# Six of eight row tiles of an output projection as block products of seven multiplications

## The chip, the cores and the metric

The kernel runs on one core of a Trainium2 chip. The metric is device time in microseconds of one execution, the median of several runs. Engines are named as the profile names them: TensorE (PE, with its weight loads PEld), VectorE (DVE), ScalarE (ACT), GpSimd (POOL) and SyncE (SP), which here only issues loads.

## The reference

A two-layer encoder works on 512 positions of 1024 channels, in float32. Each layer has an FFN, a token mixer and a second FFN, and the part that changes is the mixer's last matrix product:

```python
h = rmsnorm(x, g_mix[l])
p = h @ w_in[l]
gates = jax.nn.sigmoid(p[..., OFF_G:].astype(jnp.float32)).astype(x.dtype)
gates = gates.reshape(b, s, N_BRANCHES, d)
y_f = fourier_mix(p[..., OFF_F:OFF_B], w_fourier[l])
y_c = short_conv(p[..., OFF_B:OFF_C], p[..., OFF_C:OFF_V], p[..., OFF_V:OFF_P], w_conv[l], w_conv_out[l])
y_p = pool_mix(p[..., OFF_P:OFF_G], w_pool[l], pool_scale[l])
merged = gates[:, :, 0] * y_f + gates[:, :, 1] * y_c + gates[:, :, 2] * y_p
x = x + merged @ w_o[l]
...
h = rmsnorm(x, g_ffn2[l])
x = x + 0.5 * swiglu(h, w1_b[l], w3_b[l], w2_b[l])
```

## The kernel before

Activations lie transposed: channels on the 128 partitions, positions along the row. x is eight tiles of 128 x 512, merged likewise, and each is called a row tile. Every float32 operand is split into a high and a low part (parth and partl for weights; mergedh, unit, n and so on for activations), and a product is three matmuls: high by high, high by low, low by high (lines 362 to 364, function mm).

Most products are not made tile by tile. A job takes two output columns of the weight and pairs of row tiles, and computes the resulting 2 x 2 blocks (two row tiles by two halves of 256 positions) with seven products of blocks, M1 to M7, where a plain product needs eight. Sums of blocks replace the eighth. On the weights' side those sums are formed by VectorE in Weights.step ("sums", "rest"); on the activations' side by operands (for a normed x, tiles n) or transform (for other tiles, tiles unit). The results of the products are added by VectorE, either into temporary tiles (take) or directly to x (added). Jobs of the FFN's down projection (w2) are of the latter kind: downwards(job) says so. They use three pairs of row tiles.

run goes through the jobs. Each job issues M1 and M5, then the previous job's M4, M6, the previous job's M3, M2, M7. After the last job run issues the pieces of `after`, between them the last M4 and M3. Small pieces of VectorE and ScalarE work wait in the list `later`, of which each product issues one; a product that needs operands not yet made issues from the list until they are. A framework then orders the instructions of each engine by its own estimate and gives buffers out: 50 units of 128 x 528 in the pool act for all activations' parts.

In the mixer, jobs compute the input projection. The kinds are f, c and p for the three gates of two row tiles each, "cv" and "b" for the convolution's inputs, and "pool". Behind a gate job follow the matmuls of its branch (fourier, convolved, pooling). The function gated multiplies by the gate and adds; after gate c, rows 2i and 2i+1 of merged are complete and split_later makes their parts. The projection w_o then runs tile by tile in columns: 64 pieces (eight output columns by eight row tiles), each of three matmuls of 512 positions. The last two row tiles are held back in the first four columns. When a column is complete, finish adds it to x (line 1096), and next_norm makes the normed operand hh and hl (lines 379, 380) and the square b (line 388). POOL adds squares of columns 1 to 6 into a running sum (line 390); the buffer b has two copies.

The next FFN begins with lead: wide matmuls with hh and hl. After four row tiles of its first column it calls mean_squares (matmuls of line 404 on the summed squares, then VectorE and POOL make the norm's factor), later spread (line 430 on ScalarE) and operands (lines 476 to 494), whose tiles n the first jobs of the FFN need.

Weights come by DMA on SP's queue. A Layout fixes from an estimated time line when each is loaded and split. Kinds "raw" and "last" of a job, and chunks marked added, get their low part by a second, accumulating DMA on POOL's queue (line 207); plain chunks get it by VectorE (line 194). The projection's weights were plain chunks.

Of the kernel before, what the change touches and what calls it, by code (L numbers as in the profile page):

```python
# [13 lines left out]
ALU = mybir.AluOpType  # L14

P = 128
# [6 lines left out]
KD = D // P  # L23
# [8 lines left out]
MAXW = 1024  # L32
AW = 528
UNITS = 50
LEAD, PHASE, PLAIN = 3, 6, 18
WARM = 10


# [268 lines left out]
def encoder(ctx: ExitStack, tc: tile.TileContext, layout, x_in, w_in, consts_in, gain_in, out):  # L307
# [25 lines left out]
    def col(name, l, k):  # L333
        o = COLS[name] + l * (CW[name]) + k
        return cst[:, o : o + 1]

    def psum():
        return psp.tile([P, S], F32, tag="ps", name="ps")
# [21 lines left out]
    def mm(ps, a, b, start, stop, more=False):  # L360
        (ah, al), (bh, bl) = a, b
        nc.tensor.matmul(ps, ah, bh, start=start, stop=False, skip_group_check=more)  # L362
        nc.tensor.matmul(ps, ah, bl, start=False, stop=False, skip_group_check=more)  # L363
        nc.tensor.matmul(ps, al, bh, start=False, stop=stop, skip_group_check=more)  # L364
# [4 lines left out]
    state, later = {}, []  # L369

    ps = psum()
# [64 lines left out]
    def tt(out, a, b, op=ALU.mult):  # L436
        nc.vector.tensor_tensor(out=out, in0=a, in1=b, op=op)  # L437
# [91 lines left out]
        ))  # L529

    def downwards(job):
        return job[0][0][:2] == "w2"

    def added(job, which, ps):

# [343 lines left out]
    def mix(l, after):  # L879
# [85 lines left out]
        def gate(kind, i, rest):  # L965
            o = OFF_G + {"f": 0, "c": 1, "p": 2}[kind] * D + 2 * i * P
            job(kind, i, o, o + P, rest)

        branch = {}

        def pooling(m):
            while m // 2 not in pooled:
                one()
            branch[m] = psum()
            mm(branch[m], weights.tile(("w_pool", l, 0, m * P, P)), pooled[m // 2], True, True)

        def convolved(m, k):
            while k not in conv:
                one()
            if k == 0:  # L980
                branch[m] = psum()
            mm(branch[m], weights.tile(("w_conv_out", l, k * P, m * P, P)), conv[k], k == 0, k == 3)

        for i in range(4):
            gate("f", i, [lambda m=m: fourier(m) for m in (2 * i, 2 * i + 1)])
# [10 lines left out]
        def pool_gate(i):  # L996
            gate("p", i, [lambda m=m: pooling(m) for m in (2 * i, 2 * i + 1)])

        for do, i in (
            (pool_in, 0), (conv_in, 0), (pool_in, 2), (pool_gate, 0), (conv_in, 1), (conv_gate, 0), (pool_gate, 1),  # L1000
            (conv_in, 2), (pool_gate, 2), (conv_in, 3), (conv_gate, 2), (pool_gate, 3),
        ):
            do(i)
        for i in range(4):
            ms = (2 * i, 2 * i + 1)
            gate("c", i, [lambda m=m, k=k: convolved(m, k) for ks in ((0, 1, 2), (3,)) for m in ms for k in ks])

        def shifted(i, z):
# [13 lines left out]
        def gated(kind, m, s):  # L1022

            if kind == "f":
                tt(yf[m], yf[m], s)
            elif kind == "p":
                nc.vector.scalar_tensor_tensor(
                    out=s, in0=branch.pop(m), scalar=col("pool_scale", l, m), in1=s,
                    op0=ALU.mult, op1=ALU.mult,
                )  # L1030
                tt(yf[m], yf[m], s, ALU.add)
            else:
                tt(s, branch.pop(m), s)
                tt(s, yf.pop(m), s, ALU.add)
                split_later("merged", s, merged, m)

        def take(job, which, ps, addend, late):
            kind, i = kinds[job]
            first, c = which[0] == "1", slice(0, Q) if which[1] == "1" else slice(Q, S)
            if which == "11":  # L1040
# [54 lines left out]
        def finish(m, ps):  # L1095
            tt(x[m], ps, x[m], ALU.add)
            after(m)

        run(jobs, take, (), columns("w_o", l, merged, range(KD), finish, 4, 2), between)
        state.pop("n")  # L1100

    def next_norm(gain, l):
# [105 lines left out]
```

## Time and profile before

| what | value |
|---|---|
| runs | 2036.67, 2030.64, 2034.03 us; median 2034.03 |
| profiled execution | 2033.19 us |
| its span, first to last instruction | 2031.4 us |
| mean granted TensorE clock | 0.990 |
| projection w_o, layer 0 | 635.7 to 682.7 us of the span |
| mean matmuls behind it (line 404) | from 688.5 us |

The sums of the prediction stand against the profiled execution and are then carried over to the median of the runs. In the rows of groups, the figures after the bar are busy time and mean length of one, then the idle time before and what ended it. In rows of the timeline, the first two numbers are start and length in microseconds. A row of waits has the total, the count and the longest.

### The profile page before, as it was taken

How to read it: one execution, taken by the hardware profiler on the slowest of the kernel's cores; microseconds unless marked ns; L12 is line 12 of the kernel's file. 1: busy time of each engine (PE TensorE's matmuls, PEld its weight loads, DVE VectorE, ACT ScalarE, POOL GpSimd, SP SyncE). 2: the span in 40 equal slices, each digit the busy share in tenths (PEclk: the TensorE clock that was granted, in tenths of full speed). 3: DMA queues.
4: the chain of work that ended last, by engine and by line, in shares of the span. 5: the costliest groups of instructions: out<-in, count | busy, mean ns of one | idle time of the engine just before them, and what ended most of it. 6: DMA issues, size and time to landing. Idle time of an engine off the chain costs nothing.

```text
span 2031.4 us, 38426 instructions
## 1 busy us (share of the span) xinstructions
PE 1989.9 (98%) x14886; PEld 1898.5 (93%) x14886; DVE 1547.5 (76%) x2595; ACT 1364.6 (67%) x2250; POOL 455.5 (22%) x532
## 2 busy tenths in 40 slices
PE   8999999899999999999999999998999999999998
PEld 6899999799998899999979999988999988999997
DVE  5888887788875588888768888868897656788884
ACT  6767667776665676766667667677766556766764
POOL 3321212311110422122241212232111123121120
PEclk8999999999999999999999999999999999999999
DMA  9787878767875778787977978887787667687872
GB/s 252 155 195 172 208 165 226 160 140 168 190 174 160 155 148 195 172 207 165 228 153 152 210 166 201 183 202 154 164 182 185 164 168 141 148 209 175 194 173 89
DMA packets 145623, 358.00 MB, mean 176 GB/s; under 512 B 16160, under 2 KB 36000, under 8 KB 145440
## 3 DMA queue, kind: packets, MB, share of 16 engines
q0 software_dynamic: 59184, 149.99, 44.9%
q1 hardware_dynamic: 86112, 205.31, 31.1%
q8 instruction: 116, 1.90, 0.4%
q14 instruction: 67, 0.55, 0.1%
q10 hardware_dynamic: 144, 0.24, 0.0%
HBM read 340.80 MB, written 2.10 MB: 169 GB/s over the span
## 4 chain that ended last, share of the span: by engine, by line
PE 87%; DMA 3%; ACT 3%; issue 2%; DVE 2%; POOL 2%; POOLq 0%; SPq 0%; ACTq 0%; DVEq 0%
PE ps L363 29%; PE ps L362 29%; PE ps L364 29%; DMA n<-t 1%; DMA z<-weights 1%; DMA raw<-weights 1%; ACT parth L208 1%; ACT b L388 1%; POOL b L390 1%; DVE t L476 1%; ACT hh L379 1%; DMA w<-weights 1%; DVE t L437 0%; POOL n L489 0%; ACT partl L206 0%
## 5 line engine op out<-in xcount | busy, mean ns | idle before, releaser
L363 PE MATMUL ps<-n,parth 128*128 128x256 f32 x2760 | 779.1, 282 | 13.4 <-DMA n<-t 9.0
L362 PE MATMUL ps<-n,parth 128*128 128x256 f32 x2760 | 777.8, 282 | 5.7 <-ACT half L935 5.7
L364 PE MATMUL ps<-n,partl 128*128 128x256 f32 x2760 | 776.2, 281 | 0.0
L363 PEld LDWEIGHTS ps<-n,parth 128*128 128x128 f32 x2760 | 523.2, 190 | 16.3 <-DMA n<-t 10.3
L362 PEld LDWEIGHTS ps<-n,parth 128*128 128x128 f32 x2760 | 522.9, 189 | 7.5 <-ACT half L935 6.1
L364 PEld LDWEIGHTS ps<-n,partl 128*128 128x128 f32 x2760 | 523.0, 190 | 0.0
L207 POOL DMA_DIRECT2D part22l<-weights x163 | 143.2, 878 | 1038.5 <-ACT part22l L206 459.6
L208 ACT CAST part22h<-w 128x512 fp32r<-128x512 f32 (+1 forms) x163 | 96.1, 589 | 294.9 <-PE ps L363 198.7
L194 DVE TENSOR_TENSOR partl<-raw,parth 128x1024 fp32r<-128x1024 f32 (+3 forms) x217 | 242.8, 1121 | 40.0 <-ACT parth L193 39.7
L207 POOL DMA_DIRECT2D partl<-weights x200 | 175.9, 880 | 345.8 <-ACT partl L206 196.1
L363 PE MATMUL ps<-unit,parth 128*128 128x256 f32 x864 | 242.6, 281 | 0.0
L362 PE MATMUL ps<-unit,parth 128*128 128x256 f32 x864 | 242.6, 281 | 0.0
L364 PE MATMUL ps<-unit,partl 128*128 128x256 f32 x864 | 242.1, 280 | 0.0
L208 ACT CAST parth<-raw 128x1024 fp32r<-128x1024 f32 (+2 forms) x200 | 197.7, 988 | 50.2 <-PE ps L363 38.5
L193 ACT CAST parth<-raw 128x1024 fp32r<-128x1024 f32 (+3 forms) x217 | 207.9, 960 | 30.9 <-PE ps L363 29.4
L437 DVE TENSOR_TENSOR x<-ps,x 128x256 f32<-128x256 f32 (+1 forms) x376 | 164.0, 448 | 76.4 <-PE ps L364 76.3
L206 ACT ACTIVATE partl<-raw 128x1024 fp32r<-128x1024 f32 (+2 forms) x200 | 200.1, 1001 | 15.2 <-DMA raw<-weights 7.3
L239 DVE TENSOR_TENSOR raw<-raw,z 128x1024 f32<-128x1024 f32 (+1 forms) x163 | 186.2, 1143 | 23.0 <-ACT partl L206 16.3
L194 DVE TENSOR_TENSOR partl<-z,parth 128x1024 fp32r<-128x1024 f32 (+1 forms) x163 | 185.7, 1139 | 1.4 <-ACT parth L193 1.4
L437 DVE TENSOR_TENSOR b<-ps,sM 128x256 f32<-128x256 f32 x222 | 93.1, 420 | 117.2 <-PE ps L364 117.1
L584 ACT COPY sM<-ps 128x256 f32<-128x256 f32 x345 | 126.9, 368 | 77.0 <-PE ps L364 75.1
L193 ACT CAST parth<-z 128x1024 fp32r<-128x1024 f32 (+1 forms) x163 | 160.7, 986 | 15.1 <-PE ps L363 9.8
(188 smaller groups left out, 4052.3 us busy)
## 6 DMA issues: line engine op xcount, KB each, us to landing
raw<-weights SPq DMA_DIRECT2D x187, 512.0 KB, 4.6
partl<-weights POOLq DMA_DIRECT2D x146, 512.0 KB, 6.5
z<-weights SPq DMA_DIRECT2D x115, 256.0 KB, 3.9
w<-weights SPq DMA_DIRECT2D x115, 256.0 KB, 3.5
part22l<-weights POOLq DMA_DIRECT2D x115, 256.0 KB, 4.5
raw<-weights SPq DMA_DIRECT2D x50, 384.0 KB, 4.0
partl<-weights POOLq DMA_DIRECT2D x50, 384.0 KB, 5.7
n<-t POOLq DMA_DIRECT2D x48, 256.0 KB, 4.9
```

The lines of the kernel that those rows point to most:

```text
L193: self.nc.scalar.copy(hi[:, :w], src)
L194: self.tail.append((self.t, self.made, lambda: self.nc.vector.tensor_tensor(out=lo[:, :w], in0=src, in1=hi[:, :w].bitcast(F32), op=ALU.sub ...
L206: self.nc.scalar.activation(lo[:, :w], src, AF.Copy, scale=-1.0)
L207: self.nc.gpsimd.dma_start(lo[:, :w], self.source(key), accum_op=ALU.add)
L208: self.nc.scalar.copy(hi[:, :w], src)
L239: v.tensor_tensor(out=raw, in0=raw, in1=raws.pop(("third", key))[:, : 2 * w], op=ALU.subtract)
L362: nc.tensor.matmul(ps, ah, bh, start=start, stop=False, skip_group_check=more)
L363: nc.tensor.matmul(ps, ah, bl, start=False, stop=False, skip_group_check=more)
L364: nc.tensor.matmul(ps, al, bh, start=False, stop=stop, skip_group_check=more)
L379: nc.scalar.activation(pair[0], x[k], AF.Copy, scale=g)
L437: nc.vector.tensor_tensor(out=out, in0=a, in1=b, op=op)
L584: nc.scalar.copy(b["s" + q], ps)
```

## The change

The row tiles 0 to 5 of merged are now paired. When both tiles of a pair are complete, transform makes their seven operands, and four jobs of three pairs each (two output columns per job) are put behind the mixer's last gate job; their products are added to x by VectorE. Tiles 6 and 7 stay with columns, of which the last is held back. The gate job p 3, with its pooling, moves from before gate c 0 to before gate c 3, so the pooling and convolution results get keys of their own.

```diff
-LEAD, PHASE, PLAIN = 3, 6, 18
+LEAD, PHASE, PLAIN, MIXED = 3, 6, 18, 6
...
     def downwards(job):
-        return job[0][0][:2] == "w2"
+        return job[0][0] in ("w2_a", "w2_b", "w_o")
...
-        branch = {}
+        branch, done = {}, set()
+        state["g"] = {}
...
-            (conv_in, 2), (pool_gate, 2), (conv_in, 3), (conv_gate, 2), (pool_gate, 3),
+            (conv_in, 2), (pool_gate, 2), (conv_in, 3), (conv_gate, 2),
         ):
             do(i)
         for i in range(4):
             ms = (2 * i, 2 * i + 1)
+            if i == 3:
+                pool_gate(i)
             gate("c", i, [lambda m=m, k=k: convolved(m, k) for ks in ((0, 1, 2), (3,)) for m in ms for k in ks])
...
             else:
-                tt(s, branch.pop(m), s)
-                tt(s, yf.pop(m), s, ALU.add)
-                split_later("merged", s, merged, m)
+                tt(s, branch.pop((kind, m)), s)
+                tt(yf[m], yf[m], s, ALU.add)
+                if m >= MIXED:
+                    split_later("merged", yf.pop(m), merged, m)
+                elif m ^ 1 in done:
+                    transform(yf.pop(m & ~1), yf.pop(m | 1), state["g"], m // 2)
+                done.add(m)
 
         def take(job, which, ps, addend, late):
+            if downwards(job):
+                return added(job, which, ps)
...
-        run(jobs, take, (), columns("w_o", l, merged, range(KD), finish, 4, 2), between)
+        jobs += [(("w_o", l, m * P), ("w_o", l, (m + 1) * P), (0, MIXED // 2)) for m in range(0, KD, 2)]
+        run(jobs, take, (), columns("w_o", l, merged, range(MIXED, KD), finish, 4, 1), between)
```

On ScalarE, where the columns of layer 0's projection are finished, this is the order before. x_86 to x_93 are the row tiles 0 to 7 of x; hh is the normed operand and b the square; parth and partl are parts of weights.

```order
L379 ACTIVATE hh<-x_90,cst 128x512
L388 ACTIVATE b<-x_90 128x512
L208 CAST parth<-raw 128x1024
L206 ACTIVATE partl<-raw 128x1024
L379 ACTIVATE hh<-x_91,cst 128x512
L388 ACTIVATE b<-x_91 128x512
L193 CAST parth<-z 128x1024
L379 ACTIVATE hh<-x_92,cst 128x512
L388 ACTIVATE b<-x_92 128x512
```

And this is the same place in the changed kernel.

```order
L379 ACTIVATE hh<-x_90,cst 128x512
L193 CAST parth<-z 128x1024
L388 ACTIVATE b<-x_90 128x512
L379 ACTIVATE hh<-x_91,cst 128x512
L206 ACTIVATE partl<-raw 128x1024
L388 ACTIVATE b<-x_91 128x512
L379 ACTIVATE hh<-x_92,cst 128x512
L208 CAST parth<-raw 128x1024
L379 ACTIVATE hh<-x_93,cst 128x512
L388 ACTIVATE b<-x_92 128x512
L206 ACTIVATE partl<-raw 128x1024
L388 ACTIVATE b<-x_93 128x512
```

The squares b, which follow their operand hh directly before, now stand one to three instructions behind it, with conversions of weights between.

On VectorE, around the last gate job of layer 0, the order before is as follows: a and b are the two tiles of a gate, sM a kept product, yf the sum of the branches.

```order
L437 TENSOR_TENSOR a<-ps,sM_7929 128x256
L437 TENSOR_TENSOR b<-yf,b 128x512
L194 TENSOR_TENSOR partl<-raw,parth 128x1024
L437 TENSOR_TENSOR mergedl<-b,mergedh 128x512
L194 TENSOR_TENSOR partl<-raw,parth 128x1024
L437 TENSOR_TENSOR a<-ps,a 128x512
L437 TENSOR_TENSOR a<-yf,a 128x512
L437 TENSOR_TENSOR b<-ps,sM_7874 128x256
L437 TENSOR_TENSOR mergedl<-a,mergedh 128x512
```

In the changed kernel VectorE has this there; unit are the transform's tiles.

```order
L437 TENSOR_TENSOR a<-ps,sM_7982 128x256
L437 TENSOR_TENSOR unit<-yf,unit 128x256
L437 TENSOR_TENSOR unit<-yf,unit 128x512
L194 TENSOR_TENSOR partl<-raw,parth 128x768
L437 TENSOR_TENSOR unit<-unit 128x512
L232 TENSOR_TENSOR z<-z,w_7963 128x384
L437 TENSOR_TENSOR unit<-unit 128x512
L437 TENSOR_TENSOR unit<-yf,unit 128x256
L233 TENSOR_TENSOR z<-z,raw 128x384
L1030 SCALAR_TENSOR_TENSOR b<-ps,cst,b 128x512
```

The splits of merged (mergedl) have given way to the transforms of earlier pairs and to the sums of the new jobs' weights.

More of the change, by code (lines that the diff above doesn't have):

```diff
@@ L973, in pooling @@
                 one()
-            branch[m] = psum()
-            mm(branch[m], weights.tile(("w_pool", l, 0, m * P, P)), pooled[m // 2], True, True)
+            branch["p", m] = psum()
+            mm(branch["p", m], weights.tile(("w_pool", l, 0, m * P, P)), pooled[m // 2], True, True)
         def convolved(m, k):
@@ L980, in convolved @@
             if k == 0:
-                branch[m] = psum()
-            mm(branch[m], weights.tile(("w_conv_out", l, k * P, m * P, P)), conv[k], k == 0, k == 3)
+                branch["c", m] = psum()
+            mm(branch["c", m], weights.tile(("w_conv_out", l, k * P, m * P, P)), conv[k], k == 0, k == 3)
         for i in range(4):
@@ L1027, in gated @@
                 nc.vector.scalar_tensor_tensor(
-                    out=s, in0=branch.pop(m), scalar=col("pool_scale", l, m), in1=s,
+                    out=s, in0=branch.pop((kind, m)), scalar=col("pool_scale", l, m), in1=s,
                     op0=ALU.mult, op1=ALU.mult,
```

## The prediction

> **What bounds the kernel now.** I read the page first (busy time, chain), then TensorE's timeline for the pace of its instructions, the view of the merged tiles, a table of windows, and what TensorE waits for.
>
> ```profile
> span 2031.4 us, 38426 instructions
> PE 1989.9 (98%) x14886; PEld 1898.5 (93%) x14886; DVE 1547.5 (76%) x2595; ACT 1364.6 (67%) x2250; POOL 455.5 (22%) x532
> PE 87%; DMA 3%; ACT 3%; issue 2%; DVE 2%; POOL 2%; POOLq 0%; SPq 0%; ACTq 0%; DVEq 0%
> ```
>
> TensorE is busy for 98% of the span and holds 87% of the chain, so TensorE time saved in a stage without gaps comes off the end, as long as nothing else becomes late. Busy time is no price for a matmul, since matmuls overlap. The timeline gives the distance between starts:
>
> ```profile
> 589.76 0.28 PE L363 MATMUL ps<-n,parth 128*128 128x256 f32 x1
> ...
> 599.20 0.39 PE L362 MATMUL ps<-convh,parth 128*128 128x512 f32 x1
> ...
> 604.75 0.28 PE L362 MATMUL ps<-n,parth 128*128 128x256 f32 x1
> ```
>
> Between the first two rows stand 80 starts of 256 columns: 9.44 / 80 = 0.118 us each. Between the second and third stand 24 of 512 columns: 5.55 / 24 = 0.2315 us. The output projection runs at that pace in layer 0:
>
> ```profile
> L362 PE MATMUL ps<-mergedh,parth x64: 388/394/402, 635.7 to 682.3; 128*128 128x512 f32 x64
> L364 PE MATMUL ps<-mergedh,partl x64: 388/393/399, 636.2 to 682.7; 128*128 128x512 f32 x64
> ```
>
> 192 wide matmuls, with 24 narrow ones of the last gate job among them, start within 47.0 us: (47.0 - 24 x 0.118) / 191 = 0.231. No gap there. Next, windows: an FFN stage whose w2 products the new code copies, the stretch of the gate jobs, the projection.
>
> ```profile
> 110.00:147.00 37.00, 37.00 (x316) 37.00 (x315) 31.36 (x59) 23.36 (x35) 8.83 (x10) 1.00 0.89 210
> 573.70:635.50 61.80, 61.80 (x434) 57.59 (x433) 44.18 (x62) 37.27 (x61) 6.16 (x7) 1.00 0.67 175
> 635.50:683.00 47.50, 47.50 (x219) 39.07 (x218) 21.68 (x27) 24.63 (x34) 13.70 (x11) 1.00 0.60 150
> ```
>
> The columns are length, PE, PEld, DVE, ACT, POOL, granted clock, DMA share, GB/s. The clock is full. VectorE has 26 us to spare in the projection and 18 in the gate stretch. From 560 to 730 us TensorE waits only behind the next FFN's lead:
>
> ```profile
> PE ps L363 <- DMA n<-t: 1.7, 1, 1.7
> PE ps L363 <- DVE n L437: 1.3, 1, 1.3
> ```
>
> **The change, part by part.**
>
> TensorE. Each layer loses 48 pieces of 3 wide matmuls (six row tiles, eight columns): 144 x 0.2315 = 33.3 us. It gains 4 jobs x 7 products x 3 pairs x 3 matmuls = 252 narrow ones: 252 x 0.118 = 29.7 us. That is 3.6 us per layer and 7.2 in all. (One eighth would be 4.2; 0.6 is lost because two narrow ones take 0.236.) A rule speaks against this exchange: the Trainium skill (TensorE: Matmul & The Clock Gate, "Back-to-back issue gap") states some 131 ns for a 512-column matmul in a sustained stream. With it the removed work would be only 144 x 0.131 = 18.9 us, and the change would lose 10.8 us per layer, ending near 2055.7. The rows above measure 231 ns in this very stage, so I give that case no chance.
>
> VectorE. These rows price it (mean ns of one after the comma):
>
> ```profile
> L194 DVE TENSOR_TENSOR partl<-raw,parth 128x1024 fp32r<-128x1024 f32 x156 | 190.8, 1223 | 39.4 <-ACT parth L193 39.1
> L437 DVE TENSOR_TENSOR x<-ps,x 128x256 f32<-128x256 f32 x336 | 136.5, 419 | 43.4 <-PE ps L364 43.4
> L437 DVE TENSOR_TENSOR unit<-unit 128x512 fp32r<-128x512 f32 x108 | 74.0, 685 | 2.2 <-ACT unit L517 2.0
> L437 DVE TENSOR_TENSOR unit<-unit 128x256 f32<-128x256 f32 x144 | 57.4, 418 | 0.0
> L239 DVE TENSOR_TENSOR raw<-raw,z 128x768 f32<-128x768 f32 x48 | 45.9, 956 | 2.3 <-ACT parth L208 0.9
> L232 DVE TENSOR_TENSOR z<-z,w 128x384 f32<-128x384 f32 x48 | 26.4, 551 | 0.0
> ```
>
> Per layer: 28 additions to x at 0.42 (+11.7); weights of four jobs, each three passes of 768 columns at 0.95 and two of 384 at 0.55 (+15.8); six chunks of 1024 saved at 1.22 (-7.3); three pair transforms, each five passes of 256 and three of 512, against two passes of 512 before (+8.3). Sum +28.5 us per layer, against 44 spare (26 + 18), which hide it where they lie at the right place; were VectorE fully loaded, all 28.5 would show.
>
> The tight place lies before the first product. The unit buffers run out (28 operand tiles n stay until the last gate job), so the transforms bunch up in that job. There VectorE has 35 instructions between the "12" sum of gate c 2 and the last operand that product M1 needs. Instructions that wait for nothing overlap a little, as these three starts show (0.33 us apart, each 0.42 long):
>
> ```profile
> 698.62 0.42 DVE L437 TENSOR_TENSOR t<-t 128x256 f32<-128x256 f32 x1
> 698.95 0.42 DVE L437 TENSOR_TENSOR n<-t,n 128x256 fp32r<-128x256 f32 x1
> 699.29 1.22 DVE L239 TENSOR_TENSOR raw<-raw,z 128x1024 f32<-128x1024 f32 x1
> ```
>
> So the 35 take 18.3 us back to back (each some 0.085 less than its mean), 21.3 by the means. TensorE meanwhile has 114 narrow and 30 wide matmuls: 13.5 + 6.9 = 20.4 us. The ends are therefore 0 and 0.9 us late per layer; I take 0, because the w2 window shows VectorE 85% busy (31.36 of 37.00) with no wait on TensorE, and 18.3 / 0.85 = 21.5 would be 1.1 late at worst. In the four jobs VectorE has 28.6 us of work in TensorE's 36.0, 79%: 0. The moved gate job p 3 is the filler that makes this room; it issues the same instructions, and its loads on SP and accumulations on POOL move behind those of c 0 to c 2, as TensorE's need does. The conv products that it used to precede now follow their inputs directly, with 5.1 us of TensorE work (12 narrow of M2, 12 of M7, ten wide) against 4.2 of VectorE (two of 1024, two of 512, two of 256): 0, with a margin of only 0.9.
>
> ScalarE's rows:
>
> ```profile
> L193 ACT CAST parth<-raw 128x1024 fp32r<-128x1024 f32 x156 | 162.9, 1045 | 30.9 <-PE ps L363 29.4 <-DMA raw<-weights 0.7 <-PE ps L364 0.3
> L517 ACT CAST unit<-unit 128x512 fp32r<-128x512 f32 x108 | 65.7, 619 | 2.2 <-DVE unit L437 2.2
> L193 ACT CAST parth<-z 128x768 fp32r<-128x768 f32 x48 | 40.1, 836 | 2.1 <-PE ps L363 0.3
> ```
>
> It gains 12 casts (nine at 0.62, three at 0.42) and loses six at 0.62; each job has four weight passes of 768 at 0.84 and two of 384 (half of that, an estimate) against six of 1024 at 1.05 per layer: 3.1 + 16.8 - 6.3 = +13.6 us, into stretches where it is busy 37.27 of 61.80 and 24.63 of 47.50: 0. Neither this nor the next item removes a wait, so nothing can be gained. SP gets 6 more loads per layer. POOL gets 8 more accumulating DMAs per layer, 0.88 us of issue each:
>
> ```profile
> L207 POOL DMA_DIRECT2D partl<-weights x200 | 175.9, 880 | 345.8 <-ACT partl L206 196.1
> ```
>
> Behind them wait only later accumulations. That is 7 us on a queue busy 13.70 of 47.50, and at most the DMA share of 0.89 of the w2 window, where TensorE never waited: 0.
>
> The tail is where I see a cost. Before, each of the columns 4 to 7 took 24 wide matmuls, 5.6 us, so the squares were added at leisure. Now eight columns finish in 8.7 us (three wide, nine narrow, six wide, four times six wide after x0: 33 x 0.2315 + 1.06). POOL's six adds follow a loop: two buffers b, so the next square waits for the last add. The end of an FFN shows that loop when it is pressed, in DVE, POOL, ACT and PE rows:
>
> ```profile
> 1009.23 2.08 DVE L437 TENSOR_TENSOR x<-ps,x 128x512 f32<-128x512 f32 x3 [1.71 <-PE ps L364]
> 1016.64 1.30 POOL L390 TENSOR_TENSOR b<-b 128x512 f32<-128x512 f32 x1 [0.74 <-ACT b L388]
> 1020.82 0.63 ACT L388 ACTIVATE b<-x 128x512 f32<-128x512 f32 x1 [1.55 <-POOL b L390]
> 1027.85 1.84 PE L404 MATMUL ps<-mean,b 128*128 128x1 f32 x16
> L390 POOL TENSOR_TENSOR b<-b x6: 1298/1312/2057, 1011.8 to 1023.6; 128x512 f32<-128x512 f32 x6
> L390 POOL TENSOR_TENSOR b<-b x6: 1337/1524/1842, 660.2 to 679.7; 128x512 f32<-128x512 f32 x6
> L404 PE MATMUL ps<-mean,b x16: 166/250/250, 688.5 to 690.1; 128*128 128x1 f32 x16
> ```
>
> From the first column's addition (1009.2) to the end of the sixth add (1023.6 + 1.3) the FFN needs 15.7 us, and its mean matmuls come 3 us later. In layer 0's projection the adds ended at 681.5, 7 us ahead of 688.5. In the changed order the mean matmuls stand 28 wide matmuls behind the lead's start, so 8.7 + 6.5 - 0.2 = 15.0 us after x0. The chain needs 15.7, plus about 1.0 for one more weight conversion on ScalarE and one more DMA issue on POOL in it, which partly overlap: 16.7. TensorE runs in order, so the lead's matmuls and all that use them stand behind this wait: 1.7 us per layer, 3.4 in all. Ends: the bare loop, 2.6 + 5 x (0.74 + 1.30) + 1.3 = 14.1, gives 0; every add as long as the longest gives 1.7 + 5 x 0.75 = 5.4. What follows (spread, operands, the 3.0 us of waits behind the lead) keeps its order and its distance from the mean matmuls: 0.
>
> Sum: -7.2 + 3.4 = -3.8 us. Against the profiled execution (2033.19, span 2031.4) that is 2029.4; the median shown is 0.84 higher, so 2030.2.
>
> **The rivals.**
>
> Tail hidden. If the squares keep up, the full 7.2 us stay: 2026.8. For it speaks the FFN's 3 us of slack; against it, that columns here finish in half of an FFN's 2.8 us (twelve wide matmuls).
>
> VectorE late before the first product, which ends slower. At the tight place VectorE and ScalarE pass tiles back and forth in order. The gate jobs show such stops:
>
> ```profile
> 606.76 1.23 DVE L239 TENSOR_TENSOR raw<-raw,z 128x1024 f32<-128x1024 f32 x1 [3.10 <-ACT partl L206]
> 610.02 0.69 DVE L437 TENSOR_TENSOR a<-ps,a 128x512 f32<-128x512 f32 x1 [2.03 <-ACT a L1058]
> ```
>
> If both return there, 18.3 + 3.1 + 2.0 = 23.4 against 20.4: 3.0 us late per layer, 2036.2. It decides from 1.9 us per layer. Against it: VectorE had nothing else to do at these stops.
>
> POOL's adds lengthened by VectorE: all six at 2.06 cost 5.4 us per layer, so 2034.0 - 7.2 + 10.8 = 2037.6. One of six was that long in the FFN tail, and VectorE is denser now. The Trainium skill (SBUF — State Buffer, "Who interferes with whom") states the mechanism: a VectorE instruction with two SBUF inputs shuts out a GpSimd instruction that reads SBUF for its whole length; 2057 against 1298 ns agrees, but the other rows show that it rarely meets.
>
> The saving swallowed: if the operands behind the lead come no earlier in time, its 3.0 us of waits grow and 2034 stays. Against it: that chain starts at the mean matmuls.
>
> **How the numbers follow.** Forecast 0.50, tail hidden 0.22, VectorE late 0.15, long adds 0.08, swallowed 0.05. A measurement tells about 0.3% here, 6.1 us, from no change: faster means under 2027.9, slower over 2040.1. Faster takes the hidden tail and the forecast's own lower edge (2028.4 at 0.8 us of wait, with the runs' scatter): 0.30. Slower needs both VectorE cases together or a lateness of 5 us per layer: 0.08. The rest is 0.62. The range runs from the hidden tail less 1 us of scatter to the long adds: 2025.8 to 2037.6; the likeliest case alone, 2028.4 to 2032.
>
> **What would show it.** TensorE should start 252 unit matmuls at 0.118 in each projection; a wait of about 1.7 us should stand before the mean matmuls (L404 row, released by POOL's b), none before the first unit product; the 3.0 us behind the lead stay. I am wrong if L404 waits nothing or over 4 us, or if a wait for unit tiles of VectorE or for weights stands in the projection.

## The result and the profile after

The changed kernel takes 2049.66 us (median of 4 runs, 2047.01 to 2050.76) against 2035.32 (median of 4, 2030.64 to 2036.67): ratio 1.0071, 95% interval 1.0058 to 1.0084. It is 14 us slower, where 4 us faster was forecast. The page of the profiled execution (2049.06 us), with span, busy time by engine and the chain that ended last:

```profile
span 2047.3 us, 39127 instructions
PE 1995.0 (97%) x15102; PEld 1914.0 (93%) x15102; DVE 1598.4 (78%) x2715; ACT 1387.2 (68%) x2298; POOL 465.6 (23%) x548
PE 83%; DMA 5%; ACT 4%; DVE 3%; issue 3%; POOL 2%; POOLq 0%; SPq 0%; ACTq 0%; DVEq 0%
```

TensorE's share of the chain fell from 87% to 83%, and DMA rose from 3% to 5%. The view of the unit tiles in layer 0 shows the new products, 72 of each of the three matmuls (one of the three rows here) and 12 of each with part22, 252 in all:

```profile
L362 PE MATMUL ps<-unit,parth x72: 276/282/287, 634.7 to 671.1; 128*128 128x256 f32 x72
```

What TensorE waits for, first over the whole span (first row), then from 640 to 730 us (the others); columns are total, count, longest:

```profile
PE ps L404 <- POOL b L390: 8.9, 2, 4.5
PE ps L404 <- POOL b L390: 4.5, 1, 4.5
PE ps L363 <- DMA n<-t: 1.8, 1, 1.8
PE ps L363 <- DVE n L437: 0.7, 1, 0.7
```

From 640 to 730 us there is one new wait, 4.5 us at the mean matmuls, and another of the same size in layer 1. Behind each stands something that the profile before does not have at that place. The windows of the changed kernel, the column after POOL being the granted clock:

```profile
640.00:684.00 44.00, 44.00 (x306) 40.88 (x305) 33.68 (x62) 29.81 (x43) 14.86 (x15) 1.00 0.93 232
690.15:700.38 10.23, 10.23 (x34) 8.67 (x33) 1.19 (x3) 1.59 (x3) 1.65 (x2) 0.50 0.54 139
1697.08:1707.32 10.24, 8.84 (x29) 7.69 (x30) 3.08 (x5) 2.18 (x3) 3.58 (x3) 0.50 0.77 180
```

After TensorE has stood still, its clock is granted at half for about 10.2 us. In layer 0 all of that lies behind the wait, and 5.1 us of work are lost; in layer 1 the first 1.4 us still lie in the wait (TensorE is busy for 8.84 of 10.24), and 4.4 are lost. So: -7.2 (TensorE's saving) + 8.9 (the waits) + 9.5 (work lost at half clock behind them, both layers) = +11.2 of the 15.9 us between the two spans. Of the other 4.7 us, waits elsewhere make 1.4 (TensorE's waits over the whole span add up to 34.5 us before and 44.8 after); the rest I do not place.

The wait itself can be read from the timeline of the changed kernel, rows of PE, DVE, ACT, POOL and SP in order of time:

```profile
661.08 0.62 ACT L208 CAST part22h<-w 128x512 fp32r<-128x512 f32 x1 [3.28 <-PE ps L363]
664.17 4.11 SPq L187 DMA_DIRECT2D raw<-weights  x3
669.51 0.40 PE L364 MATMUL ps<-mergedh,partl 128*128 128x512 f32 x1
672.22 0.69 DVE L233 TENSOR_TENSOR z<-z,raw 128x512 f32<-128x512 f32 x1 [5.93 <-DMA raw<-weights]
672.83 1.61 DVE L437 TENSOR_TENSOR x<-ps,x 128x256 f32<-128x256 f32 x3
673.88 0.72 ACT L379 ACTIVATE hh<-x,cst 128x512 fp32r<-128x512 f32 x1 [3.55 <-DVE x L437]
676.34 1.80 POOL L390 TENSOR_TENSOR b<-b 128x512 f32<-128x512 f32 x1 [2.25 <-DVE x L437]
687.95 1.61 POOL L390 TENSOR_TENSOR b<-b 128x512 f32<-128x512 f32 x1 [0.74 <-ACT b L388]
689.61 0.38 PE L404 MATMUL ps<-mean,b 128*128 128x1 f32 x2 [4.55 <-POOL b L390]
```

Column 0 is complete on TensorE at 669.9 (669.51 + 0.40), and TensorE is ready for the mean matmuls at 689.61 - 4.55 = 685.1, 15.2 us later. VectorE adds that column to x0 only at about 673.2 (the second of the three instructions of the row at 672.83): ahead of it in VectorE's order stands L233, a weight sum for the next FFN's first job, which waited 5.9 us for a load. From 673.2 to the end of the last add (689.56) the chain of squares takes 16.4. And 3.3 + 16.4 - 15.2 = 4.5.

### The profile page after: what moved, and what is told of

Read it like the earlier page. It is cut to its first block, busy times and chain, and to the rows that moved or that the text cites. A ratio compares the mean times of both kernels' runs of the same rounds, so it can differ in the third digit from the quotient of the medians.

```text
span 2047.3 us, 39127 instructions
## 1 busy us (share of the span) xinstructions
PE 1995.0 (97%) x15102; PEld 1914.0 (93%) x15102; DVE 1598.4 (78%) x2715; ACT 1387.2 (68%) x2298; POOL 465.6 (23%) x548
## 4 chain that ended last, share of the span: by engine, by line
PE 83%; DMA 5%; ACT 4%; DVE 3%; issue 3%; POOL 2%; POOLq 0%; SPq 0%; ACTq 0%; DVEq 0%
PE ps L363 27%; PE ps L362 27%; PE ps L364 27%; DMA raw<-weights 2%; DMA n<-t 1%; POOL b L390 1%; DMA z<-weights 1%; ACT b L388 1%; ACT parth L208 1%; ACT hh L379 1%; ACT partl L206 1%; DMA w<-weights 1%; POOL n L489 0%; DVE t L476 0%; DVE t L437 0%
## 5 line engine op out<-in xcount | busy, mean ns | idle before, releaser
L207 POOL DMA_DIRECT2D part22l<-weights x171 | 149.9, 877 | 1059.5 <-ACT part22l L206 444.7
L362 PE MATMUL ps<-unit,parth 128*128 128x256 f32 x1008 | 283.4, 281 | 0.0
L363 PE MATMUL ps<-unit,parth 128*128 128x256 f32 x1008 | 283.2, 281 | 0.0
L364 PE MATMUL ps<-unit,partl 128*128 128x256 f32 x1008 | 282.9, 281 | 0.0
L194 DVE TENSOR_TENSOR partl<-raw,parth 128x1024 fp32r<-128x1024 f32 (+3 forms) x213 | 236.0, 1109 | 37.4 <-ACT parth L193 37.4
L437 DVE TENSOR_TENSOR x<-ps,x 128x256 f32<-128x256 f32 (+1 forms) x432 | 185.7, 444 | 54.1 <-PE ps L364 53.8
L208 ACT CAST parth<-raw 128x1024 fp32r<-128x1024 f32 (+2 forms) x208 | 204.1, 981 | 25.8 <-PE ps L363 11.2
L206 ACT ACTIVATE partl<-raw 128x1024 fp32r<-128x1024 f32 (+2 forms) x208 | 206.8, 995 | 15.7 <-PE ps L363 7.9
L239 DVE TENSOR_TENSOR raw<-raw,z 128x1024 f32<-128x1024 f32 (+1 forms) x171 | 194.0, 1134 | 21.9 <-ACT partl L206 11.7
L194 DVE TENSOR_TENSOR partl<-z,parth 128x1024 fp32r<-128x1024 f32 (+1 forms) x171 | 195.1, 1141 | 3.4 <-ACT parth L193 3.1
L363 PEld LDWEIGHTS ps<-unit,parth 128*128 128x128 f32 x1008 | 190.0, 189 | 0.3
L362 PEld LDWEIGHTS ps<-unit,parth 128*128 128x128 f32 x1008 | 190.0, 188 | 0.2
L364 PEld LDWEIGHTS ps<-unit,partl 128*128 128x128 f32 x1008 | 189.9, 188 | 0.0
```

The source lines that it names most:

```text
L194: self.tail.append((self.t, self.made, lambda: self.nc.vector.tensor_tensor(out=lo[:, :w], in0=src, in1=hi[:, :w].bitcast(F32), op=ALU.sub ...
L206: self.nc.scalar.activation(lo[:, :w], src, AF.Copy, scale=-1.0)
L207: self.nc.gpsimd.dma_start(lo[:, :w], self.source(key), accum_op=ALU.add)
L208: self.nc.scalar.copy(hi[:, :w], src)
L239: v.tensor_tensor(out=raw, in0=raw, in1=raws.pop(("third", key))[:, : 2 * w], op=ALU.subtract)
```

## The experiments

Each is a variant of the changed kernel, unless it says otherwise. Ratios are to the kernel before on the same chip, with 95% intervals.

**e1. Fill the wait.** Twenty matmuls that nothing reads stand ahead of the mean matmuls.

```diff
             if n == at["factor"]:
+                if s == "_b":
+                    spare = psum()
+                    for _ in range(20):
+                        nc.tensor.matmul(spare, h[3][0][:, :P], h[3][0], start=True, stop=True)
                 mean_squares()
```

> Computes the same, plus 20 matmuls of 512 columns per layer (0.2315 us each, 4.6 us together, results unused) that TensorE issues just before the mean matmuls behind the projection, where the changed kernel waits 4.6 us. Theory A (the wait of over 4 us makes the granted clock fall to 0.5 for 10.2 us, which costs 5.1 us per layer): no wait of over 1 us is left at L404, the clock stays at 1.00 behind it, and the time is about 2049.7 - 10.2 = 2039.5 us. Rival B (the clock falls because of what is computed there, not because of the wait): clock 0.5 and 2049.7 us as before.

The trace bears out the mechanism: with 0.3 us left of the wait, the clock is at 1.00 where it was 0.50 from 690.15 on (windows of e1, layer 0):

```profile
689.80:695.00 5.20, 4.61 (x28) 3.89 (x28) 2.21 (x4) 1.56 (x2) 2.34 (x3) 1.00 0.96 223
695.00:700.00 5.00, 5.00 (x25) 4.09 (x24) 1.93 (x4) 1.97 (x3) 0.00 (x0) 1.00 0.30 108
```

Its span is 2039.1, 8 us below the change's. But the profiled execution is the fastest of six: the median is 2048.15, ratio 1.0053 (1.0035 to 1.0071). What the other five lost is not seen, so the time stays inconclusive, and the clock needed another test (e14). In layer 1 some 0.9 us of waits were left, and 3.4 us at half clock followed.

**e2. A third buffer b.**

```diff
-        return tmp.tile([P, S], F32, tag=tag, name=tag, bufs=2)[:, :w]
+        return tmp.tile([P, S], F32, tag=tag, name=tag, bufs=3 if tag == "b" else 2)[:, :w]
```

> Three buffers b instead of two, so the next square need not wait for the add before it. Theory C (the loop of squares and adds sets the wait at the mean matmuls): adds follow each other at 1.4 us instead of 2.1, the wait falls from 4.6 to about 1.3 us, the clock does not fall: 2049.7 - 2 x (3.3 + 5.1) = 2032.9 us. Rival D (VectorE's stop before a weight sum, 5.9 us for a load, sets it, since it delays the additions to x): wait about 4 us, 2048 us or more.

2040.07 us, ratio 1.0018 (1.0002 to 1.0034). Its waits from 640 to 730 us:

```profile
PE ps L404 <- POOL b L390: 2.6, 1, 2.6
PE ps L363 <- DVE n L437: 2.6, 1, 2.6
```

So the loop of two buffers is part of the wait, but over half of it stays.

**e3. The sums later.** The first job of the next FFN plans its loads and sums 18 us later, which moves VectorE's L233 behind the additions to x.

```diff
-            early = 22.0 if t["M1"] > before + 20.0 else 0.0
+            early = (4.0 if job[0][0] == "w3_b" else 22.0) if t["M1"] > before + 20.0 else 0.0
```

> The weights of the first job behind the second FFN's lead are planned 18 us later, so that VectorE's sum with the late load (L233) stands behind all eight additions to x. Theory D (VectorE's stop delays the columns by about 3 us): first addition 3 us earlier, wait at the mean matmuls about 1.7 us, no clock fall: 2049.7 - 2 x (2.9 + 5.1) = 2033.7 us, plus up to 3 us per layer where that job now waits for its weights. Rival C (the loop alone): wait still 4 us or more, 2048 us.

2050.6 us, ratio 1.0067 (1.0041 to 1.0093). The waits, 640 to 730 us:

```profile
PE ps L363 <- DVE hl L380: 1.8, 1, 1.8
PE ps L404 <- POOL b L390: 0.9, 1, 0.9
```

L233 now stands in front of hl of the last tiles. The stop was moved, not removed.

**e4. Two pairs.** Four row tiles in block products, four in columns.

```diff
-LEAD, PHASE, PLAIN, MIXED = 3, 6, 18, 6
+LEAD, PHASE, PLAIN, MIXED = 3, 6, 18, 4
```

> Four row tiles of eight (two pairs) as block products, four as columns. Each column's end is 12 wide matmuls, 2.8 us, as at the end of an FFN. TensorE saves 96 x 0.2315 - 168 x 0.118 = 2.4 us per layer. If the short columns make the wait (theory C or D), the wait is under 1 us, the clock stays, and the time is 2035 - 4.8 = 2030 us. If the block products themselves slow the stage or the clock (rival B), two thirds of the loss stay: 2045 us.

2060.62 us, ratio 1.0112 (1.0096 to 1.0129): a miss. VectorE's timeline:

```profile
673.65 0.69 DVE L233 TENSOR_TENSOR z<-z,raw 128x512 f32<-128x512 f32 x1 [8.25 <-DMA raw<-weights]
```

The wait for that load is 2.3 us longer than in the change, and TensorE waits 5.2 us at L404 in all (4.1 for POOL's b and 1.1 for ScalarE's). That pointed away from the length of the tail and to the loads.

**e5. No stop on VectorE.** The sum L233 of that first job reads a block that has landed in place of the one that it needs.

```diff
             v.tensor_tensor(out=z[:, w : 2 * w], in0=z[:, 2 * w : 3 * w],
-                in1=first[:, :w], op=ALU.subtract)
+                in1=(w22 if key[0][0] == "w3_b" and key[0][2] == LEAD * P else first)[:, :w], op=ALU.subtract)
```

> The changed kernel with one operand replaced: the weight difference of the next FFN's first job (L233) is taken from a block that has long landed instead of the late one, so VectorE has nothing to wait for ahead of x0's addition (one weight block of one job per layer is therefore wrong). Theory: of the 4.6 us at the mean matmuls, 16.7 - 15.0 = 1.7 are the chain of squares itself and 2.9 are VectorE's stop ahead of x0; without the stop the L404 wait is 1.7 us per layer, the clock falls for one 3.4 us stretch at most, and the time is 0 to 4 us under the kernel before (ratio 0.998 to 1.000). Rival: the two buffers of b and slow POOL adds make the wait; then it stays over 4 us with 10 us of half clock behind it, ratio 1.006.

2053.83 us, ratio 1.0076 (1.0062 to 1.0090); the wait stayed at 4.4 us. The timeline says why (DVE and ACT rows of e5):

```profile
669.66 1.39 DVE L437 TENSOR_TENSOR x<-ps,x 128x512 f32<-128x512 f32 x2 [0.27 <-PE ps L364]
672.15 0.62 ACT L388 ACTIVATE b<-x 128x512 f32<-128x512 f32 x1
676.23 1.06 ACT L206 ACTIVATE partl<-raw 128x1024 fp32r<-128x1024 f32 x1 [3.46 <-DMA raw<-weights]
677.19 0.71 ACT L379 ACTIVATE hh<-x,cst 128x512 fp32r<-128x512 f32 x1
```

x0 is added at 669.7, 3.5 us sooner. Two squares follow at once, and then ScalarE stands for 3.46 us at a conversion of the lead's weights whose load has not landed, with the third hh behind it. It starts at 677.2; in the change, at 677.3 as well. VectorE's stop had only covered ScalarE's. Both wait for loads of the same few microseconds.

**e6. The mean matmuls later.** Three row tiles of the lead (18 wide matmuls, 4.2 us) go ahead of them.

```diff
+            if s == "_b":
+                at.update(factor=7, spread=9, operands=(10, 12, 15, 19))
```

> The changed kernel with the mean matmuls, spread and operands of the second FFN's lead three row tiles (18 wide matmuls, 4.2 us) later in TensorE's order. Theory: what is late is the chain that the mean matmuls start, not their place. The wait at L404 falls to about 0.5 us and the clock stays up there, but TensorE then has 4.2 us less work behind them, and the waits at the lead's end grow from 2.8 to about 7 us per layer, with a fall of the clock there instead: 2044 to 2050, ratio 1.004 to 1.007. Rival: only the place is wrong; waits at both places end under 3 us per layer, ratio under 1.000.

2037.25 us, ratio 1.0001 (0.9990 to 1.0013): my theory fell and the rival came near. Its waits, 640 to 730 us:

```profile
PE ps L363 <- DMA n<-t: 2.1, 1, 2.1
PE ps L363 <- DVE hl L380: 2.1, 1, 2.1
PE ps L363 <- DVE n L437: 0.6, 1, 0.6
```

The waits at the lead's end did not grow (2.7 together, 2.5 in the change), so the chain behind the mean matmuls had some 4 us of slack. What is left is 2.1 us for hl.

**e7. Columns earlier.** Wide pieces of columns 0 to 3 stand between the block jobs, columns 4 to 7 last.

```diff
+        pieces = columns("w_o", l, merged, range(MIXED, KD), finish, 0, 1)
+        for n in (2, 3):
+            between[jobs[n - 4]] = [pieces.pop(0) for _ in range(4)]
+        run(jobs, take, (), pieces, between)
```

> The changed kernel with the wide pieces of columns 0 and 1 put behind the third block job of the projection, those of columns 2 and 3 behind the fourth, and columns 4 to 7 last, whole. Same arithmetic. Theory: four of the eight squares are then added during the jobs, so POOL's chain ends before TensorE reaches the mean matmuls: no wait at L404, no fall of the clock there, and the 7.2 us of TensorE time come through: 5 to 8 us under the kernel before, ratio 0.996 to 0.998. Rival: merged 6 and 7 or the wide pieces' weights come too late for the earlier place, and a wait moves into the projection: ratio 1.000 to 1.006.

2048.19 us, ratio 1.0060 (1.0048 to 1.0073). (As written, columns 6 and 7 are normed before the last job's M3 is added to them; the amount of work is the same.) The L404 wait was 5.3 us. Squares that begin earlier do not help as long as the later ones stand behind the same loads.

**e8. The moved gate job alone**, in the kernel before.

```diff
-            (conv_in, 2), (pool_gate, 2), (conv_in, 3), (conv_gate, 2), (pool_gate, 3),
+            (conv_in, 2), (pool_gate, 2), (conv_in, 3), (conv_gate, 2),
...
+            if i == 3:
+                pool_gate(i)
             gate("c", i, ...)
```

> The kernel before with one part of the change alone: gate job p 3 moved from before gate c 0 to before gate c 3; the projection stays in plain columns. Theory: it issues the same instructions and removes no wait, so within 3 us of the kernel before (ratio 0.9985 to 1.0015). Rival: the moved job delays loads or conversions in the gate stretch, 2 us or more per layer (ratio over 1.002).

2036.90 us, ratio 1.0001 (0.9989 to 1.0013). That part costs nothing.

**e9. VectorE in place of the accumulating DMAs** for the projection's jobs.

```diff
+        if key[0] != "chunk" and key[1][0][0] == "w_o":
+            self.nc.scalar.copy(hi[:, :w], src)
+            self.nc.vector.tensor_tensor(out=lo[:, :w], in0=src, in1=hi[:, :w].bitcast(F32), op=ALU.subtract)
+            return hi, lo
```

> The changed kernel with the low parts of the projection's job weights made by VectorE (high part subtracted) instead of the accumulating DMAs: 2.25 MB fewer per projection, eight fewer issues on POOL and eight fewer low parts on ScalarE, 6 us more of VectorE work. Theory: DMA is what makes the tail late; without these bytes the load on which ScalarE stood 3.46 us (676.2 in e5) lands about 7 us earlier at some 300 GB/s, the wait at L404 falls to 1 to 2 us per layer, no fall of the clock: 1 to 6 us under the kernel before (ratio 0.997 to 1.000). Rival: VectorE, busy 9.7 of each 10 us in the jobs, becomes late; waits of unit products or of the x additions appear in the projection, ratio over 1.004.

2055.73 us, ratio 1.0084 (1.0069 to 1.0099): the rival's ratio, though of the waits that it named only one stands in the projections (0.6 us for a unit tile, layer 1). Windows of e9, the fourth time being VectorE's busy time and the last but one column the DMA share:

```profile
640.00:650.00 10.00, 10.00 (x87) 10.00 (x86) 10.00 (x20) 6.33 (x10) 0.00 (x0) 1.00 0.21 69
650.00:660.00 10.00, 10.00 (x87) 10.00 (x87) 9.98 (x20) 3.76 (x5) 0.00 (x0) 1.00 0.35 113
```

VectorE is full in the jobs. But DMA is idle for two thirds of that time, and L233 still waited for its load until 679.3. That put in doubt that the jobs' traffic makes the loads late.

**e10. Plain weights in the lead.** Its first 12 steps take their low parts by VectorE.

```diff
-                mm(ps, weights.tile(spec, added=not first or n >= 12), h[k], k == 0, k == KD - 1)
+                mm(ps, weights.tile(spec, added=(n >= 12 if s == "_b" else not first or n >= 12)), h[k], k == 0, k == KD - 1)
```

> The changed kernel with the first 12 row-tile steps of the second FFN's lead taking their weights' low parts by VectorE (as plain chunks) instead of the accumulating DMA: 1.5 MB fewer per layer in the tail and three ScalarE passes of 1.04 us fewer, three VectorE passes of 1.22 more, in the tail itself. Theory: ScalarE's queue holds fewer conversions between the squares and DMA is freer: the L404 wait falls by 2 to 4 us per layer and the half clock with it, ratio 0.998 to 1.003. Rival: the squares' loop on two buffers sets the pace whatever ScalarE does between them: wait over 4 us, ratio 1.006.

2038.03 us, ratio 1.0004 (0.9993 to 1.0016; one execution of 7249.7 us, far off the rest, does not touch the median). DVE, POOL and PE rows of its timeline:

```profile
671.06 0.69 DVE L233 TENSOR_TENSOR z<-z,raw 128x512 f32<-128x512 f32 x1 [0.32 <-DMA raw<-weights]
671.67 1.61 DVE L437 TENSOR_TENSOR x<-ps,x 128x256 f32<-128x256 f32 x3
686.84 1.60 POOL L390 TENSOR_TENSOR b<-b 128x512 f32<-128x512 f32 x1 [0.74 <-ACT b L388]
688.49 0.38 PE L404 MATMUL ps<-mean,b 128*128 128x1 f32 x2 [1.56 <-POOL b L390]
```

With the load there in time, the chain still takes 16.4 us (672.0 to 688.44) and the wait is 1.6: near the 16.7 and the 1.7 that the prediction had worked out. The clock behind it misses 0.17 of 10 us, which is 3.4 us at half, against 10.2 (behind layer 1's wait of 1.5 us there is none):

```profile
690.00:700.00 10.00, 10.00 (x47) 8.32 (x46) 4.74 (x11) 3.66 (x7) 2.01 (x2) 0.83 0.46 110
```

**e11. e2 and e6 together.**

> The changed kernel with both a third buffer b and the mean matmuls three row tiles later. The first alone gave waits of 2.8 and 2.1 us at L404, the second alone none there but 2.3 and 2.5 us on hl in the lead. Theory: hl is late because ScalarE makes hh between squares that wait for b; with three b the hh come 0.5 us apart sooner, the wait for hl falls under 1 us, nothing waits at L404: 3 to 6 us under the kernel before, ratio 0.997 to 0.9985. Rival: the load that ScalarE waits for sets the time of hh; the wait for hl stays 2 us and the ratio 1.000.

2037.47 us, ratio 0.9999 (0.9989 to 1.0010): the rival's ratio, by another wait than either theory named. Nothing waits at L404 or for hl; a wait for the norm's factor took their place (waits of e11):

```profile
PE ps L422 <- DVE a L411: 2.8, 1, 2.8
```

In VectorE's order L233 stands ahead of that factor, and waited 4.7 us for its load there.

**e12. e9 and e11 together.**

> e11 with the edit of e9 as well (no accumulating DMAs for the projection's jobs). If DMA is what makes the tail late, no wait is left in the tail and the 7.2 us come through, with up to 2 us of longer waits at the lead's end: ratio 0.996 to 0.998. If VectorE becomes late, it shows as waits before unit products, and the ratio is over 1.000 and above that of e11.

2047.75 us, ratio 1.0051 (1.0037 to 1.0065): VectorE late again, as in e9. In layer 0 its weight sum waited 4.9 us for the load, until 677.3, and TensorE waited 4.1 us for the norm's factor.

**e13. The jobs' accumulating DMAs left out.** Nothing replaces them.

```diff
-        self.nc.gpsimd.dma_start(lo[:, :w], self.source(key), accum_op=ALU.add)
+        if key[0] == "chunk" or key[1][0][0] != "w_o":
+            self.nc.gpsimd.dma_start(lo[:, :w], self.source(key), accum_op=ALU.add)
```

> The changed kernel without the accumulating DMAs of the projection's job weights (their low parts are then wrong; nothing takes over the work): 2.25 MB and eight POOL issues fewer per layer, VectorE and ScalarE as before. Theory A, the DMA traffic of the jobs makes the next FFN's loads late: VectorE's wait at L233 ahead of x0 and ScalarE's wait at its partl fall under 1 us, the L404 wait to 1.7 us, ratio 0.998 to 1.001. Theory B, the loads are late because their buffers come free late (e9 had DMA nearly idle from 640 to 660 us and L233 still waited 5.5 us): the waits at L233 or at partl stay over 3 us, the L404 wait over 4 us, ratio 1.005 to 1.007.

2053.17 us, ratio 1.0077 (1.0063 to 1.0091): theory B. From 640 to 660 us 2.51 MB move instead of 4.12, yet both engines still stop: ScalarE for 3.15 us, and VectorE for 2.88 us until 671.5, where it was 5.93 us until 672.2 in the change (ACT and DVE rows of e13; line numbers are one higher from 208 on):

```profile
678.70 1.06 ACT L206 ACTIVATE partl<-raw 128x1024 fp32r<-128x1024 f32 x1 [3.15 <-DMA raw<-weights]
671.50 0.69 DVE L234 TENSOR_TENSOR z<-z,raw 128x512 f32<-128x512 f32 x1 [2.88 <-DMA raw<-weights]
```

The L404 wait is 4.3 us. The traffic of the new jobs is not the cause.

**e14. Standing still, in the kernel before.** Each column of the second FFN's lead begins with row tile 7, the last one normed.

```diff
-            order = [(f, k) for f in range(LEAD) for k in range(KD)]
+            ks = [KD - 1, *range(KD - 1)] if s == "_b" else range(KD)
+            order = [(f, k) for f in range(LEAD) for k in ks]
```

> The kernel before, with one edit: in the second FFN's lead each column begins with row tile 7, the last to be normed, so TensorE must stand still for it right after the projection, some 3.4 us per layer (hl of x7 is ready near 686.4, TensorE comes at 682.9). Nothing is added to any engine. Theory: standing still costs more than itself, since the clock is then granted at half for 3.4 to 10 us: 5 to 8 us per layer, 10 to 16 in all (ratio 1.005 to 1.008), with segments of 0.5 right behind each wait. Rival: the clock falls of the changed kernel have another cause, and the wait costs itself: 6.8 us in all, ratio 1.003 and no fall there.

2047.86 us, ratio 1.0055 (1.0038 to 1.0072). TensorE's wait, from 670 to 720 us:

```profile
PE ps L362 <- ACT hh L379: 2.5, 1, 2.5
```

and the windows of the wait and behind it, with layer 1's in the last row:

```profile
682.14:685.55 3.41, 0.93 (x5) 0.42 (x4) 0.75 (x2) 2.70 (x4) 0.29 (x1) 1.00 0.00 0
685.55:695.79 10.24, 10.24 (x32) 8.79 (x33) 1.89 (x4) 0.43 (x1) 1.62 (x2) 0.50 0.45 104
1692.51:1702.75 10.24, 10.24 (x32) 8.79 (x33) 1.91 (x4) 0.46 (x1) 1.64 (x2) 0.50 0.47 102
```

Nothing was added to the kernel before; two waits of 2.5 us, 5 in all, cost 10.1 at the median (7.7 to 14.7). About 10.2 us at half clock follow each, which is 5.1 us of work lost; with the waits that makes 15.2, near the 15.3 between the two profiled spans (2046.7 and 2031.4), and the median shows less. The lower end of the interval is above the waits alone. Standing still is what lowers the clock, though not every wait of this length does (last section).

**e15. e10, a third b, and the mean matmuls two row tiles later.** To the edits of e2 and e10 comes:

```diff
+            if s == "_b":
+                at.update(factor=6, spread=8, operands=(9, 12, 15, 19))
```

> The changed kernel with three edits, each of which shortened the wait alone: lead's first 12 steps plain (e10), a third b (e2), mean matmuls two row tiles later (e6 had three). Theory: e10 left 1.7 us at L404 and no other new wait; two row tiles are 2.8 us, so nothing waits at L404, no clock falls there, and 3.4 us of waits and 1.7 of half clock come off e10: 4 to 6 us under the kernel before, ratio 0.997 to 0.9985. Rival: the next late thing takes over, L233 in front of rtok or hl in the lead, as in e6 and e11: ratio 1.000.

2027.54 us (2024.15 to 2032.31), ratio 0.9952 (0.9937 to 0.9967): this version beats both kernels. One wait is left from 640 to 730 us:

```profile
PE ps L363 <- DMA n<-t: 2.7, 1, 2.7
```

and POOL's timeline shows five adds in a row, 1.6 us each, where they came every 2.3 us on average:

```profile
672.47 8.09 POOL L390 TENSOR_TENSOR b<-b 128x512 f32<-128x512 f32 x5
```

**e16. The whole lead plain, mean matmuls two row tiles later, two b.** The last edit of e15, and in e10's line:

```diff
-added=(n >= 12 if s == "_b" else not first or n >= 12)
+added=(n >= 24 if s == "_b" else not first or n >= 12)
```

> The changed kernel with all 24 steps of the second FFN's lead plain and the mean matmuls two row tiles later, two buffers b. 3 MB fewer by DMA and six ScalarE passes fewer per layer than the change, six VectorE passes of 1.22 more, half of them behind the tail where VectorE is half idle. Theory: as e15, ratio 0.996 to 0.9985, with the waits at the lead's end shorter by up to 1 us, since fewer transfers run there. Rival: VectorE's passes delay the operands n and lengthen the waits at the lead's end by 2 us or more: ratio 1.000 to 1.003.

2039.14 us, ratio 1.0008 (0.9997 to 1.0018): no gain. Its waits in layer 0's tail are small (0.6 us for hl). In the profiled executions TensorE waits 39.0 us in all, against 33.2 in e15, and its mean granted clock is 0.987 against 0.992, some 10 us of work; so much of what it lost is half clock, spread over the span. Why the clock fell more often is not shown.

**e17. The three edits of e15 in the kernel before.**

> The kernel before with the three edits of e15 (lead's first 12 steps plain, a third b, mean matmuls two row tiles later) and without the change. Theory: there was no wait in its tail to remove, so it stays within 4 us of the kernel before (ratio 0.998 to 1.002), and most of e15's 10 us is the 7.2 us of TensorE time that the change saves. Rival: the three edits are a gain of their own (fewer transfers and ScalarE passes in the lead): ratio 0.995 to 0.997, and the change gives nothing even then.

2033.56 us, ratio 0.9985 (0.9974 to 0.9996). The edits are worth 3.6 us by themselves, and with the change 10.2 (e15), each against the kernel before on its own chip. The 6.6 between them are near the 7.2 that the change saves on TensorE, but the two intervals leave some 4 us either way.

**e18. e15 with two b.**

> e15 with the two buffers b of the change. Theory: e10 left 1.7 us at L404 with two b, and two row tiles are 2.8 us, so nothing waits there either, and the time is that of e15 (ratio 0.994 to 0.998). Rival: with two b the squares hold ScalarE back, hl comes late in the lead as in e6 (2.3 us and 2.5 us), or L233 stands in front of rtok: ratio 0.998 to 1.001.

2032.29 us, ratio 0.9983 (0.9972 to 0.9995). A wait of 0.3 us is left at L404 and hl is in time, yet the time is 4.9 us under the kernel before, against 10.2 in e15. No single wait carries those 5 us: in the profiled executions all waits together are 2.2 us longer than in e15 (35.4 against 33.2), and the mean granted clock is 0.990 against 0.992, some 4 us of work. That the loop of two b is behind this is not shown.

## Why the prediction was wrong, point by point

**TensorE, 7.2 us saved: right.** The 252 narrow matmuls ran from 634.7 to 671.4 beside wide ones without a gap (44.00 of 44.00 us busy), at 0.118 us, and e15 against e17 shows 6.6 us of it as time, within some 4.

**VectorE ahead of the first product, 0: right.** No wait for unit tiles stands in the projection, and VectorE was busy for 28.33 of 36.70 us in the jobs (634.70 to 671.40), where 28.6 of 36.0 were forecast. The moved gate job, 0: right (e8).

**DMA issues and loads, 0: the first step that failed.** They were costed at nothing because TensorE had never waited in a window with as much DMA. But VectorE and ScalarE take loads in their own order, and in the tail both stood for one, 5.9 us ahead of x0 in the change and 3.5 us among the squares in e5. The prediction asked only whether TensorE waits for weights.

**The tail, 1.7 us per layer: mis-sized, 4.5.** Both of its lengths were right: 15.0 us on TensorE and 16.7 in the chain were forecast, 15.2 and 16.4 measured. Its starting point was wrong. It let the chain start when TensorE completes column 0; it started 3.3 us later, when a load landed. With that load in time (e10) the wait is 1.6.

**A missing term: the clock.** The prediction took TensorE at full clock behind the wait, and gave the price of a wait as its length. Each wait brought 10.2 us at half clock, 5.1 us more in layer 0 and 4.4 in layer 1. Even a wait of the forecast size may not be free of it: behind e10's 1.6 us, layer 0 lost another 1.7 (3.4 us at half), behind 1.5 us in layer 1 nothing. That a wait of 2.5 us alone can do it is shown by e14.

**The waits at the lead's end stay: right** (3.0 before, 2.5 after). None of the rivals that had a chance came: the dearest of them, long adds, was 12 us too low.

**Why the loads are late** can be read from how long they take. SP sends three loads of 512 KB from 664.17 on, the first of which L233 waits for, and POOL sends three accumulating DMAs for the lead's own weights among them. The time from issue to landing (median) is as follows: loads and accumulating DMAs of the change (664 to 669 us), then the same three loads in e10 and in e13 (666 to 671 us each):

```profile
raw<-weights SPq DMA_DIRECT2D x3, 512.0 KB, 10.1
partl<-weights POOLq DMA_DIRECT2D x3, 512.0 KB, 11.2
raw<-weights SPq DMA_DIRECT2D x3, 512.0 KB, 4.4
raw<-weights SPq DMA_DIRECT2D x3, 512.0 KB, 10.2
```

In e10 the first of them goes out no earlier (5.4 us before column 0 is complete on TensorE, 5.7 in the change), but the lead's accumulating DMAs are not there, and the loads land in time. In e13 only those of the jobs are missing, and two of the three loads are as slow as before. So the loads are slowed on their way, by the lead's own accumulating DMAs and not by the new jobs' traffic. Why these come so close together is open. ScalarE stood 3.28 us at part22h until TensorE gave its buffer back, and made three of the lead's low parts within 6 us behind that; whether the two part22 buffers of the new jobs begin this chain was not tried.

## What to carry to other kernels

When work on the busiest engine is shortened ahead of a chain that hangs on it, ask for each engine in that chain what stands in front of the link in its order, and when the load of that instruction lands; a transfer that the busiest engine never waits for may still stop two others. Price a wait of TensorE with the clock behind it: here its length and, where half clock followed, half of the 3.4 to 10.2 us that it lasted. And before giving up a change that saves work, look for what takes its place: three small edits in the tail turned 14 us lost into some 10 gained, of which 3.6 are the edits' own (e17).

## What the runs showed of the hardware

The half clock came in pieces of about 3.4 us: one behind a wait of 1.6 us (e10), three behind 2.5 (e14) and with 4.5 (the change), although TensorE was busy again. The Trainium skill (TensorE: Matmul & The Clock Gate, "What's actually happening") states that an idle window of about 3.4 us returns the array to half clock, and that one busy window releases it. The size of the pieces agrees; both the threshold and the length differ here, since waits shorter than a window were enough and 10.2 us followed.

The length of a wait alone does not decide. In each trace all stretches at half clock begin and end on one fixed grid with steps of 3.41 us. These are steps of that grid: three in the kernel before, around a wait of 3.3 us from 1389.6, and two in e15, around its wait of 2.7 us (the first number after the comma is TensorE's busy time):

```profile
1388.14:1391.56 3.42, 1.50 (x7) 0.92 (x5) 3.42 (x9) 3.11 (x6) 0.86 (x1) 1.00 1.06 196
1391.56:1394.97 3.41, 1.94 (x13) 1.74 (x14) 3.41 (x5) 3.08 (x6) 0.86 (x1) 1.00 1.03 172
1394.97:1398.38 3.41, 3.41 (x30) 3.41 (x29) 3.41 (x8) 2.69 (x4) 0.00 (x0) 1.00 0.43 146
715.36:718.77 3.41, 2.08 (x18) 1.87 (x16) 2.24 (x5) 2.06 (x5) 3.41 (x3) 1.00 0.93 171
718.77:722.19 3.42, 2.06 (x16) 2.01 (x17) 2.88 (x7) 0.70 (x1) 0.01 (x1) 1.00 0.64 113
```

Both waits are split between two steps, 1.9 and 1.5 us, 1.3 and 1.4 us, and no half clock follows. The 2.5 us of e14 lie in one step (682.14 to 685.55), and the next three are at half. Counted over the 20 traces here: of the steps at full clock in which TensorE stood idle for 2.0 us or more, all 147 were followed by half clock; of those with 1.35 to 2.0 us 43 of 125; of those with 0.9 to 1.35 us none of 63. Six steps with less idle time were followed by it too, the one of e10 among them, and each holds 10 to 16 mean matmuls, which write a single column; a step of the kernel before with 16 of these was not. What sets the number of steps at half, one to four here, stays open.
